# Layer 1's two query products ahead of its keys, the latent stream normalized ahead of layer 0's overflow loop, and one expert job in four f32 passes

## The chip, the core and the metric

The kernel runs on one core of a Trainium2 chip. The metric is device time in microseconds (us), median of several runs; smaller is better. TensorE is called PE here, VectorE DVE, ScalarE ACT, GpSimdE POOL, and SP is the engine whose queue issues most of the loads from HBM.

## What is computed

Two layers act on a residual stream of 256 latent tokens and 256 context tokens, each 1024 wide. The parts that matter here, cut from the reference:

```python
# layer 0: attention and Fourier groups, then a mixture of experts for 512 tokens
ff = moe_ffn(jnp.concatenate([h2, hc2], axis=0), *moe_args)     # 64 experts, top 8, one shared expert
ctx = layer_norm(DN_ALPHA * ctx + cg2 * ff_ctx, ln2_g[l], ln2_b[l])
x = layer_norm(DN_ALPHA * x + g2 * ff_lat, ln2_g[l], ln2_b[l])
# layer 1: neighbourhood attention; the latents ask, latents and context answer
h  = x * (1.0 + sc1) + sh1
hc = ctx * (1.0 + csc1) + csh1
q, k, v = jnp.split(h_lat @ w_in, 3, axis=-1)
kc, vc = jnp.split(h_ctx @ w_in[:, NA_WIDTH:], 2, axis=-1)
```

All arithmetic is in f32 accuracy. Layer 1's queries come from the latents alone (256 columns), its keys and values from latents and context (512 columns).

## The kernel before, in words

**Layer 0's experts.** `moe` walks through 42 jobs (0 to 41) of 128 slots. A job holds one expert (a single), or two (a pair, 64 slots each). Its PE work is the gate and up product (`gate_up`, L1337), the transposes of the next job's input and of its own activation, the down product (`down`, L1351), and scatter matmuls (L1544) that place earlier results at their tokens. Singles after the third job go another way: `gate_up3` and `down3` split each f32 operand into a high part (a cast on ACT) and a low part (a subtraction on DVE), by `split` at L161, and `mm3` (L165 to L167) multiplies in three fp32r passes: high by high, low by high, high by low. The list `passes` says which way a job goes. Job 39 is a single, the last one; jobs 38, 40 and 41 are pairs. The weights come through a pool of 11 tiles of 1 MB (`w8`), which SP's queue refills as PE or DVE let go of them.

**The end of layer 0.** After job 41 four scatter pieces are added to the latents' residual `xt[0:2]` by DVE, `stats` takes their mean and variance, and four scatter pieces of the context are added to `acc[2:4]` by DVE (L1434). `post` brings two slices of layer 1's modulation to column form. Then comes `overflow_blocks`, a loop on the device for experts with more tokens than slots; it runs zero times here, but all engines meet at its branch (L1642). After the loop `normalize` (L1896) brings the latents to their normalized form.

**Layer 1's mixer.** `mixer_na` reads six slices of `na_w_in`: `na[0]`, `na[1]` are the queries of heads 0 to 3 and 4 to 7, `na[2]`, `na[3]` the keys, `na[4]`, `na[5]` the values. `project` multiplies one slice in four steps of 24 matmuls by `mm3`; for each step `prefetch` splits a quarter of the slice (`wh` on ACT, `wl` on DVE) one step ahead, and a `tick` after each step does other work. `turn` transposes a quarter of the stream, scales it (`hTf`, L429 and L430), and splits it (`hT`). The order is: query 0, key 0, value 0, query 1, key 1, value 1. `fold_ctx` (L1889, L1890) and a second `normalize` finish the context beside query 0. `attention` does one unit (a head and half of the queries) for each `next(g)`: a score matmul (L910), softmax on DVE and ACT, four transposes (L493) two units later and four matmuls with the values (L920) one unit after that; its 11 steps for the first four heads lie in the ticks of query 1, key 1 and value 1, one in each.

SP and PE run in the order in which the code is written (`manual_schedule`); DVE, ACT and POOL are ordered by the scheduler.

Of the kernel before, what the change touches and what calls it, by code (L numbers as in the profile page):

```python
# [22 lines left out]
D = 1024  # L23
# [95 lines left out]
def tile_block(ctx: ExitStack, tc: tile.TileContext, I, out):  # L119
# [25 lines left out]
    def k4(shape, name="k4", dt=F32):  # L145
        return keep.tile(shape, dt, name=name, tag="k4", bufs=NK4)
# [366 lines left out]
    def project(w, out_mm, tick, n=4, eng=V, nxt=None, within=None):  # L513


        ps = [bank() for _ in range(n)]
        for jj in range(0, NJ, 2):
            prefetch(w, jj, eng)
            wh, wl = ready_parts.pop((id(w), jj))
            if nxt:  # L520
                if jj + 2 < NJ:
                    prefetch(w, jj + 2, eng)
                elif nxt() is not None:
                    prefetch(nxt(), 0, eng)
            for i in range(n):
                for j in range(2):
                    out_mm(ps[i], i, jj + j, wh[:, j], wl[:, j])
                if within:
                    next(within)
            tick()  # L530
        return ps

    def token_major(h):
        def f(p, i, j, wh, wl):
            sl = slice(i * 128, i * 128 + 128)
            mm3(p, h(0, j, sl), h(1, j, sl), wh, wl, j == 0, j == NJ - 1)
        return f
# [326 lines left out]

    def mixer_na(mp):
        load = na.pop("load")
        na[2], na[4], na[1] = load(2), load(4), load(1)
        st = Stream(2)
        mod_stream(st, 1, range(6, 12), mod_rows,
                   lambda shape: mp.tile(shape, F32, name="mh", tag="mh", bufs=2))  # L870
# [9 lines left out]
        yT = []  # L880
        kv, qT = {}, {}

        def fill(n, steps):

            steps = iter(steps)
            tick = lambda: next(steps)()
            qT[n] = k4([128, 4, 256], "qT")
            ps = project(na[n], channel_major(h, 256), tick, nxt=lambda: na[2 + n])
            del na[n]
            for i in range(4):  # L890
                A.activation(qT[n][:, i], ps[i][:, :256], AF.Copy, scale=SCALE)
            kv[n] = [w8([128, 4, 512], "kv") for _ in range(2)]
            ps = project(na[2 + n], channel_major(h, 512), tick, nxt=lambda: na[4 + n])
            del na[2 + n]
            for i in range(4):
                A.copy(kv[n][0][:, i], ps[i])
            if n == 0:
                na[3] = load(3)
            ps = project(na[4 + n], token_major(h), tick, nxt=lambda: na.get(1))
            del na[4 + n]  # L900
            for i in range(4):
                A.copy(kv[n][1][:, i], ps[i])
            if n == 0:
                na[5] = load(5)
# [30 lines left out]
                    late = attend(*units[i - 2], sms.pop(i - 2))  # L935
                yield

        busy(3)
        for jj in range(2):
            last = turn(0, jj)  # L940
        busy(3)
        prefetch(na[0], 0)
        with tc.issue_after(last[0].ins), tc.issue_after(last[1].ins):
            fold_ctx()
            prefetch(na[0], 2)
            prefetch(na[0], 4, G)
        with tc.issue_after(last[1].ins):
            normalize(Stats(mp, 2).of(xt[2:]), xt[2:])
        order.clear()
        g = attention([(0, hh, t) for hh in range(4) for t in range(2)])  # L950

        def turns(*a):
            for s, jj in a:
                turn(s, jj)
        tail = lambda: next(g, None)
        with tc.issue_after(last[0].ins), tc.issue_after(last[1].ins):
            fill(0, [lambda: turns((0, 2), (0, 3)), lambda: None, lambda: turns((1, 0), (1, 1)),
                     lambda: turns((1, 2), (1, 3))] + [st.tick] * 8)
        del xt[2:]
        yT.extend(k4([128, 4, 256], "yT") for _ in range(2))  # L960

        def both_():
            st.tick()
            tail()
        fill(1, [both_] * 4 + [tail] * 8)
        for _ in g:
            pass
        del kv[0], qT[0]
# [91 lines left out]
    def moe(l, out_of, nt, mp, pre=lambda: None, post=lambda: None):  # L1060
# [356 lines left out]
        def stats():  # L1417

            x_stats.of(xt[0:2], True)
            if l:  # L1420
                y_out.extend(k4([128, D], "y_out") for _ in range(2 - len(y_out)))
                finish1(x_stats, *after, y_out)

        def fold(g2s):
# [216 lines left out]
        def overflow_blocks():  # L1641
            with tc.For_i(0, n_blk.pop()) as i:  # L1642
# [18 lines left out]
                sl1 = mp.tile([128, 1, 5], F32, name="sl1", tag="sl1")  # L1661
                V.tensor_copy(sl1[:, 0], p[:, :5])
                slot_info(sl1, w1, t1, i1)
                x1 = k4([128, D], "x1")
                V.memset(x1, 0.0)
                gather(x1, i1)
                tr = slots_T(x1, 4)
# [7 lines left out]

        passes = []
        for sg_ in jobs:
            passes.append(3 if l == 0 and len(sg_) == 1 and len(passes) > 2 else 4)
        grp, sc = [], iter(())
        over = overflow()  # L1680
        LA = 3 if l == 0 else 2
        with tc.manual_schedule(engines={mybir.EngineType.SP, mybir.EngineType.PE}):
# [186 lines left out]
            if l:  # L1869
                last_job(njob - 1, sc, g2s[0], add_x)  # L1870
                after.extend(spread(lnc[:, k]) for k in range(2))
                stats()
            else:
                for _ in range(4):
                    next(sc)
                stats()
                with tc.issue_after(x_stats.last.ins):
                    for _ in sc:
                        pass
            post()  # L1880

        overflow_blocks()
        return x_stats, y_out

    g2c = []

    def fold_ctx():
        for t in (2, 3):
            V.tensor_mul(acc[t], acc[t], g2c[0])  # L1889
            V.tensor_add(xt[t], xt[t], acc[t])  # L1890
        g2c.clear()
# [41 lines left out]

    mix0.close()
    with tc.tile_pool(name="moe0", bufs=1) as mp:
        normalize(moe(0, out0, 4, mp, preload_na, mods_na)[0], xt[:2])
    with tc.tile_pool(name="mix1", bufs=1) as mp:
        with tc.manual_schedule(engines={mybir.EngineType.SP, mybir.EngineType.PE}):
            out1 = mixer_na(mp)
# [91 lines left out]
```

## Time and profile before

| | us |
|---|---|
| median of 3 runs | 1667.28 (1667.20 to 1667.38) |
| the profiled execution's own time | 1667.79 |
| its span | 1666.0 |
| PE busy | 1560.8 (94%) |
| DVE, ACT, POOL busy | 762.9, 444.3, 174.0 |
| moved by DMA | 547.91 MB, 329 GB/s over the span |

Layer 0's experts end at about 936 us of the span, where the loop's branch is; layer 1's mixer goes on to about 1100, and layer 1's experts to the end. The profiled execution took 0.5 us more than the median. Busy times of a matmul are modelled, so spacings between matmuls are read from their starts. An f32 matmul shows as two records, an fp32r matmul as one.

### The profile page before, as it was taken

What the parts mean: (1) busy time and instruction counts of PE and PEld (TensorE: products, weight loads), DVE (VectorE), ACT (ScalarE), POOL (GpSimd) and SP (SyncE); (2) the same over time, 40 slices, a digit from 0 to 9 for tenths busy, and PEclk for the clock granted to TensorE, in tenths of its full rate; (3) what the DMA queues carried; (4) which work ended last, traced back from release to release, by engine and by line L of the source; (5) the groups of instructions that cost most, each with busy time, mean ns of one, the idle gap of its engine ahead of it and who ended that gap; (6) DMA issues with size and microseconds to landing.
All of it is one profiled execution on the core that took longest, in us unless ns stands there. A gap on an engine that the chain in (4) does not pass through costs nothing. (4 is left out here: it accounts for less than half of the span.)

```text
span 1666.0 us, 30733 instructions
## 1 busy us (share of the span) xinstructions
PE 1560.8 (94%) x12138; PEld 1005.9 (60%) x12138; DVE 762.9 (46%) x2077; ACT 444.3 (27%) x882; POOL 174.0 (10%) x162
## 2 busy tenths in 40 slices
PE   7999999999999999999998799999999988989995
PEld 5765687546556566565665577866756654546542
DVE  2475585425455445354566832347443422223225
ACT  2447311113132232232222243332222211112111
POOL 1003210123221121221110000011000000000000
PEclk9999999999999999999999899999999999999998
DMA  9947864799999999989998566247779999999994
GB/s 331 340 172 290 297 233 162 268 366 382 346 398 345 402 401 389 392 327 406 404 407 309 205 212 222 89 181 309 303 316 420 419 419 419 419 420 419 419 420 179
DMA packets 122819, 547.91 MB, mean 329 GB/s; under 512 B 12917, under 2 KB 21509, under 8 KB 74672
## 3 DMA queue, kind: packets, MB, share of 16 engines
q1 hardware_dynamic: 108032, 501.76, 75.6%
q0 software_dynamic: 14640, 44.15, 8.6%
q8 instruction: 97, 1.59, 0.4%
q14 instruction: 50, 0.41, 0.1%
HBM read 532.10 MB, written 21.58 MB: 332 GB/s over the span
## 5 line engine op out<-in xcount | busy, mean ns | idle before, releaser
L1337 PE MATMUL bank<-w,xT 128*32 128x256 f32 (+1 forms) x5696 | 462.8, 388 | 25.8 <-DMA w<-in_moe_w_up_dram 20.2
L1337 PEld LDWEIGHTS bank<-w,xT 128*32 128x32 f32 (+1 forms) x5696 | 276.5, 122 | 204.9 <-DMA w<-in_moe_w_up_dram 28.2
L1351 PE MATMUL bank<-w,aT 128*32 128x512 f32 (+2 forms) x1248 | 235.3, 599 | 3.0 <-ACT aT L1312 2.9
L1293 DVE SCALAR_TENSOR_TENSOR a<-s,wsl,bank 128x256 f32<-128x256 f32 x70 | 33.6, 480 | 407.4 <-ACT s L1292 407.4
L1292 ACT ACTIVATE s<-bank 128x256 f32<-128x256 f32 x70 | 26.9, 385 | 544.5 <-PE bank L1337 496.7
L1544 PE MATMUL bank<-yy,ss 128*128 128x512 f32 x560 | 159.0, 411 | 1.4 <-DVE yy L161 1.1
L1536 DVE TENSOR_TENSOR acc<-acc,bank 128x512 f32<-128x512 f32 x212 | 138.0, 683 | 43.3 <-PE bank L1544 41.6
L1351 PEld LDWEIGHTS bank<-w,aT 128*32 128x32 f32 (+2 forms) x1248 | 68.5, 123 | 120.0 <-issue 104.0
L1544 PEld LDWEIGHTS bank<-yy,ss 128*128 128x128 f32 x560 | 97.3, 191 | 25.9 <-DVE yy L161 5.0
L161 DVE TENSOR_TENSOR yy<-bank,yy 128x512 fp32r<-128x512 f32 x96 | 65.9, 689 | 91.7 <-ACT yy L161 91.7
L161 ACT CAST yy<-bank 128x512 fp32r<-128x512 f32 x96 | 56.2, 586 | 161.6 <-PE bank L1351 144.2
L1445 POOL DMA_INDIRECT xg<-h2d,idx x42 | 52.1, 1239 | 356.8 <-PE bank L1459 181.7
L161 DVE TENSOR_TENSOR wl<-half,wh 128x1024 fp32r<-128x1024 f32 x35 | 42.7, 1224 | 74.4 <-ACT wh L161 74.4
L1250 DVE TENSOR_SCALAR oh<-ib,pos 128x64 bf16<-128x64 bf16 (+3 forms) x432 | 68.7, 245 | 9.7 <-PE bank L1276 9.7
L1516 POOL DMA_INDIRECT accd<-yd,idx x37 | 59.4, 1605 | 128.0 <-issue 92.7
L165 PE MATMUL bank<-wh,hT 128*128 128x512 f32 x160 | 65.2, 407 | 1.7 <-ACT wh L161 1.1
L167 PE MATMUL bank<-wl,hT 128*128 128x512 f32 x160 | 63.4, 396 | 0.5 <-DVE wl L161 0.5
L166 PE MATMUL bank<-wh,hT 128*128 128x512 f32 x160 | 63.2, 395 | 0.3 <-DVE hT L161 0.2
L1485 PE MATMUL bank<-ohr,h2p 128*128 128x256 f32 x448 | 60.8, 289 | 0.0
L1485 PEld LDWEIGHTS bank<-ohr,h2p 128*128 128x128 f32 x448 | 55.3, 191 | 8.2 <-PE bank L1337 4.4
L1437 POOL TENSOR_TENSOR xr<-xr,tmp 128x512 f32<-128x512 f32 x2 | 3.3, 1649 | 478.2 <-DVE tmp L1436 478.2
L1459 PE MATMUL bank<-head,xg 128*128 128x128 f32 x336 | 52.1, 278 | 0.0
(362 smaller groups left out, 2313.2 us busy)
## 6 DMA issues: line engine op xcount, KB each, us to landing
w<-in_moe_w_gate_dram SPq DMA_DIRECT2D x128, 1024.0 KB
w<-in_moe_w_up_dram SPq DMA_DIRECT2D x128, 1024.0 KB
w<-in_moe_w_down_dram SPq DMA_DIRECT2D x104, 1024.0 KB
w<-in_w_mod_dram SPq DMA_DIRECT2D x24, 1024.0 KB
half<-in_na_w_in_dram SPq DMA_DIRECT2D x12, 1024.0 KB
mh<-in_w_mod_dram SPq DMA_DIRECT2D x12, 1024.0 KB
w<-in_w_mod_dram SPq DMA_DIRECT2D x16, 512.0 KB
row<-rowsd POOLq DMA_DIRECT2D x15, 512.0 KB, 8.3
```

The lines of the kernel that those rows point to most:

```text
L161: return A.copy(o_h, src), eng.tensor_sub(o_l, src, o_h.bitcast(F32))
L165: T.matmul(p, xh, wh, start=first, stop=False)
L166: T.matmul(p, xl, wh, start=False, stop=False)
L167: T.matmul(p, xh, wl, start=False, stop=last)
L1250: V.tensor_scalar(oh[:, 32 * lane:32 * (lane + m)], ib[:, off:off + 32 * m], pos[:, t, c:c + 1], None, op0=OP.is_equal)
L1337: T.matmul(p[sl, q * FF:q * FF + FF], xT(j, sl), ws[k][0][q][:, j], start=j == 0, stop=j == NJ - 1, **kw)
L1351: T.matmul(p[sl], aT[:, j, sl], d[:, n * 512:n * 512 + 512], start=j == 0, stop=j == 1, **kw)
L1445: G.indirect_dma_start(out=x, out_offset=None, in_=h2d[:n2, :], in_offset=bass.IndirectOffsetOnAxis(ap=idx_col, axis=0), bounds_check=n2 - ...
L1485: T.matmul(o, h2p[t][k][:, 2 * q + j], oh[:, t].rearrange("p a b -> p (a b)")[:, :n], start=t == 0 and k == 0, stop=t == nt - 1 and k == 1)
L1516: G.indirect_dma_start(out=accd[turn_[0]][:, :], out_offset=bass.IndirectOffsetOnAxis(ap=i_, axis=0), in_=y[32 * lane:32 * (lane + m)], in ...
L1536: add = {0: lambda t, r, p: V.tensor_add(acc[t][:, r], acc[t][:, r], p)}
L1544: T.matmul(p, ss[:, t * 128:t * 128 + 128], yy[:, q, r], start=k == 0 and q == 0, stop=k == len(grp) - 1 and q == 1)
```

## The change

- `passes`: the last three jobs are no longer eligible for three passes, so job 39 runs as `gate_up` and `down` in plain f32 (four passes inside PE), without splits of its input, weights and activation.
- The end of layer 0: the context's four last pieces are copied by ACT from PSUM to a tile `late` of the pool `w8`; `post` comes ahead of `stats`; `stats` also writes the normalized latents to two new tiles `y_out`, ahead of the loop, which take the place of `xt[0:2]`. `fold_ctx` adds `late` to `acc` first. In the loop's body `x1` moves to another pool.
- The mixer: `fill` loses its query product to `queries`. The order is now query 0, query 1, key 0, value 0, key 1, value 1; the loads of slices follow it. `fold_ctx` and the context's `normalize` come after the first step of query 0, with a square root on ACT in place of one on DVE; the first context quarters are turned in the ticks of query 1. Three warm-up matmuls go, and no split is given to POOL any more. In value 1 each tick takes two attention steps (`two_tails`).

```diff
-        na[2], na[4], na[1] = load(2), load(4), load(1)
+        na[1], na[2], na[4] = load(1), load(2), load(4)
...
-        def fill(n, steps):
+        def queries(n, steps, nxt):
 
             steps = iter(steps)
-            tick = lambda: next(steps)()
             qT[n] = k4([128, 4, 256], "qT")
-            ps = project(na[n], channel_major(h, 256), tick, nxt=lambda: na[2 + n])
+            ps = project(na[n], channel_major(h, 256), lambda: next(steps)(), nxt=lambda: na[nxt])
             del na[n]
             for i in range(4):
                 A.activation(qT[n][:, i], ps[i][:, :256], AF.Copy, scale=SCALE)
+
+        def fill(n, steps):
+
+            steps = iter(steps)
+            tick = lambda: next(steps)()
...
-            ps = project(na[4 + n], token_major(h), tick, nxt=lambda: na.get(1))
+            ps = project(na[4 + n], token_major(h), tick, nxt=lambda: na.get(3))
...
-        busy(3)
         for jj in range(2):
             last = turn(0, jj)
         busy(3)
         prefetch(na[0], 0)
         with tc.issue_after(last[0].ins), tc.issue_after(last[1].ins):
-            fold_ctx()
             prefetch(na[0], 2)
-            prefetch(na[0], 4, G)
-        with tc.issue_after(last[1].ins):
-            normalize(Stats(mp, 2).of(xt[2:]), xt[2:])
...
+        def rest():
+
+            turn(0, 2)
+            last = turn(0, 3)
+            with tc.issue_after(last[1].ins):
+                fold_ctx()
+                normalize(Stats(mp, 2).of(xt[2:], True), xt[2:])
...
-            fill(0, [lambda: turns((0, 2), (0, 3)), lambda: None, lambda: turns((1, 0), (1, 1)),
-                     lambda: turns((1, 2), (1, 3))] + [st.tick] * 8)
+            queries(0, [rest, none, none, none], 1)
+        queries(1, [none, none, lambda: turns((1, 0), (1, 1)), lambda: turns((1, 2), (1, 3))], 2)
+        fill(0, [st.tick] * 8)
...
-        fill(1, [both_] * 4 + [tail] * 8)
+
+        def two_tails():
+            tail()
+            tail()
+        fill(1, [both_] * 4 + [two_tails] * 4)
...
-            if l:
-                y_out.extend(k4([128, D], "y_out") for _ in range(2 - len(y_out)))
+            y_out.extend(k4([128, D], "y_out") for _ in range(2 - len(y_out)))
+            if l == 0:
+                for t in range(2):
+                    mu, rs = x_stats[t]
+                    V.tensor_scalar(y_out[t], xt[t], mu, rs, op0=OP.subtract, op1=OP.mult)
+            else:
                 finish1(x_stats, *after, y_out)
...
-            passes.append(3 if l == 0 and len(sg_) == 1 and len(passes) > 2 else 4)
+            passes.append(3 if l == 0 and len(sg_) == 1 and 2 < len(passes) < njob - 3 else 4)
...
+                add_x = add[0]
+                late.append(w8([128, 2, D], "late"))
+                add[0] = lambda t, r, p: A.copy(late[0][:, t - 2, r], p)
+                for _ in sc:
+                    pass
+                add[0] = add_x
+                post()
                 stats()
-                with tc.issue_after(x_stats.last.ins):
-                    for _ in sc:
-                        pass
-            post()
 
         overflow_blocks()
+        if l == 0:
+            xt[:2] = y_out
...
     def fold_ctx():
+        y = late.pop()
         for t in (2, 3):
+            V.tensor_add(acc[t], acc[t], y[:, t - 2])
             V.tensor_mul(acc[t], acc[t], g2c[0])
             V.tensor_add(xt[t], xt[t], acc[t])
...
-        normalize(moe(0, out0, 4, mp, preload_na, mods_na)[0], xt[:2])
+        moe(0, out0, 4, mp, preload_na, mods_na)
```

What this does to the engines' orders is seen at three places. The first is PE in job 39. In the program before, its down product is twelve matmuls that alternate between the parts (`wh`, `wl` of the weights, `aTh`, `aTl` of the activation):

```order
L1544 MATMUL bank<-yy,ss 128x512 x4
L165 MATMUL bank<-wh,aTh 128x512
L166 MATMUL bank<-wh,aTl 128x512
L167 MATMUL bank<-wl,aTh 128x512
L165 MATMUL bank<-wh,aTh 128x512
...
L1544 MATMUL bank<-yy,ss 128x512 x8
```

In the changed program the whole job reads so on PE:

```order
L1350 MATMUL bank<-w_8772,xT 128x256 x8
L1350 MATMUL bank<-w_8774,xT 128x256 x8
L1476 MATMUL bank<-head,xg_1854 128x128 x4
L1561 MATMUL bank<-yy,ss 128x512 x4
L1321 MATMUL bank<-head,a 128x128 x2
L1476 MATMUL bank<-head,xg_1854 128x128 x4
L1561 MATMUL bank<-yy,ss 128x512 x4
L1364 MATMUL bank<-w_8776,aT 128x512 x4
L1561 MATMUL bank<-yy,ss 128x512 x8
```

Forty-eight matmuls of the gate and up product have become 16, and twelve of the down product four; the transposes and scatters between them stand as they did.

The second place is DVE right after the loop's branch. Before, it starts with the latents' normalization and has the context's fold (L1889, L1890) ahead of query 0's second low part:

```order
L1896 TENSOR_SCALAR xr_9103<-xr_9103,mv,rs 128x1024
L1896 TENSOR_SCALAR xr_9105<-xr_9105,mv,rs 128x1024
L161 TENSOR_TENSOR wl<-half,wh 128x1024
L430 TENSOR_SCALAR hTf<-bank,acol_1807,bcol_1808 128x256 x2
L161 TENSOR_TENSOR hT<-hTf,hT 128x2x256 x2
L1889 TENSOR_TENSOR acc_2623<-acc_2623,row 128x1024
L1889 TENSOR_TENSOR acc_2754<-acc_2754,row 128x1024
L1890 TENSOR_TENSOR xr_9107<-xr_9107,acc_2623 128x1024
L1890 TENSOR_TENSOR xr_9109<-xr_9109,acc_2754 128x1024
L161 TENSOR_TENSOR wl<-half,wh 128x1024
```

In the changed program:

```order
L161 TENSOR_TENSOR wl<-half,wh 128x1024
L430 TENSOR_SCALAR hTf<-bank,acol_1807,bcol_1808 128x256 x2
L161 TENSOR_TENSOR hT<-hTf,hT 128x2x256 x2
L161 TENSOR_TENSOR wl<-half,wh 128x1024 x3
L430 TENSOR_SCALAR hTf<-bank,acol_1807,bcol_1808 128x256 x2
L161 TENSOR_TENSOR hT<-hTf,hT 128x2x256 x2
L1912 TENSOR_TENSOR acc_2623<-acc_2623,late 128x1024
...
L1914 TENSOR_TENSOR xr_9041<-xr_9041,acc_2754 128x1024
...
L459 BN_STATS st<-xr_9041 128x6
L161 TENSOR_TENSOR wl<-half,wh 128x1024
```

All four low parts of query 0 and all four turned quarters of the latents now stand ahead of the fold; the last `wl` shown is the first low part of query 1, and it stands behind six 1024-wide operations of the fold and four statistics.

The third place is PE in value 1, after its first step, where a tick takes two attention steps (`ps` is a softmax's result, `PT` its transpose on ACT, `kv` the keys or values):

```order
L914 MATMUL bank_10404<-kv_9818,qT_9496 128x512
L924 MATMUL bank_10414<-PT_10361,kv_9819 128x128 x4
L493 MATMUL bank_10421<-head_69,ps_10296 128x128 x4
L914 MATMUL bank_10427<-kv_9818,qT_9496 128x512
L924 MATMUL bank_10437<-PT_10420,kv_9819 128x128 x4
L493 MATMUL bank_10444<-head_69,ps_10347 128x128 x4
```

The transposes of `ps_10296` fill the bank from which `PT_10420` is copied, and the second step's four value matmuls read that copy with one score matmul between; `ps_10347` belongs to the score of the tick before.

## Rows read from the trace of the kernel before

**Rows 1.** The page, moved bytes in 40 equal slices of the span.

```profile
GB/s 331 340 172 290 297 233 162 268 366 382 346 398 345 402 401 389 392 327 406 404 407 309 205 212 222 89 181 309 303 316 420 419 419 419 419 420 419 419 420 179
```

**Rows 2.** Windows: length, PE, PEld, DVE, ACT, POOL busy, PEclk, DMA share, GB/s.

```profile
847.23:862.92 15.69, 15.69 (x107) 9.67 (x107) 9.95 (x17) 5.27 (x9) 2.13 (x3) 1.00 1.02 421
862.92:887.72 24.80, 18.31 (x88) 15.32 (x86) 16.88 (x22) 6.42 (x10) 1.05 (x2) 0.79 0.87 344
907.12:935.93 28.81, 22.18 (x139) 10.90 (x138) 20.36 (x37) 4.97 (x10) 0.00 (x0) 0.91 0.36 133
935.93:963.38 27.45, 21.94 (x139) 20.00 (x140) 23.05 (x43) 12.65 (x21) 3.19 (x1) 0.84 1.01 376
963.38:1100.00 136.62, 136.62 (x731) 103.20 (x730) 43.95 (x78) 47.60 (x83) 1.09 (x2) 1.00 0.43 148
```

**Rows 3.** Timeline of PE in job 39: start, length, instructions [idle before, releaser].

```profile
866.37 0.58 PE L167 MATMUL bank<-wl,xT 128*128 128x256 f32 x1 [3.06 <-DVE wl L161]
878.31 0.49 PE L166 MATMUL bank<-wh,aTl 128*128 128x512 f32 x1 [1.60 <-DVE aTl L161]
880.64 0.80 PE L167 MATMUL bank<-wl,aTh 128*128 128x512 f32 x1 [1.83 <-DVE wl L161]
```

**Rows 4.** Timeline of DVE in job 39.

```profile
865.09 2.36 DVE L161 TENSOR_TENSOR wl<-w,wh 128x1024 fp32r<-128x1024 f32 x2
```

**Rows 5.** Timeline of PE in layer 1's shared expert, f32 products of one expert's shape.

```profile
1148.26 7.13 PE L1389 MATMUL bank<-w,h2T 128*128 128x256 f32 x32
1161.68 3.60 PE L1351 MATMUL bank<-w,aT 128*128 128x512 f32 x8
```

**Rows 6.** Windows, columns as above.

```profile
880.00:890.00 10.00, 9.36 (x40) 6.89 (x42) 5.49 (x8) 1.17 (x2) 0.00 (x0) 0.67 0.42 145
```

**Rows 7.** The tile ad (context sums fetched from DRAM): issue to landing.

```profile
DMA to landing us min/median/max: 14.8/14.8/14.8
```

**Rows 8.** Timeline around the loop's branch; the last row is from the kernel's end.

```profile
932.36 2.47 DVE L1434 TENSOR_TENSOR acc<-acc,bank 128x512 f32<-128x512 f32 x4
935.62 1.04 ACT L161 CAST wh<-half 128x1024 fp32r<-128x1024 f32 x1 [4.00 <-DVEq L1642]
935.93 1.65 PE L274 MATMUL bank<-onesf 128*128 128x128 f32 x6 [3.79 <-DVEq L1642]
937.03 1.53 DVE L1896 TENSOR_SCALAR xr<-xr,mv,rs 128x1024 f32<-128x1024 f32 x2 [2.20 <-ACT wh L161]
937.90 0.48 PE L425 MATMUL bank<-head,xr 128*128 128x128 f32 x1 [0.32 <-DVE xr L1896]
...
1649.12 2.05 ACT L394 COPY spread<-bank 128x512 f32<-128x512 f32 x4 [2.22 <-PE bank L393]
```

**Rows 9.** Timeline of DVE after the loop.

```profile
940.16 0.54 DVE L430 TENSOR_SCALAR hTf<-bank,acol,bcol 128x256 f32<-128x256 f32 x1 [0.46 <-ACT hTf L429]
941.52 1.42 DVE L161 TENSOR_TENSOR hT<-hTf,hT 128x512 fp32r<-128x512 f32 x2
942.85 2.35 DVE L1889 TENSOR_TENSOR acc<-acc,row 128x1024 f32<-128x1024 f32 x2
948.53 1.87 DVE L459 BATCH_NORM_STATS2 st<-xr 128x6 f32<-128x512 f32 x3
```

**Rows 10.** Timeline of PE in query 0, at its second step.

```profile
948.67 0.39 PE L166 MATMUL bank<-hT,wl 128*128 128x256 f32 x1 [2.52 <-DVE wl L161]
```

**Rows 11.** Timeline of PE in query 1: first and last of the 24 matmuls of a step.

```profile
1017.93 0.39 PE L165 MATMUL bank<-hT,wh 128*128 128x256 f32 x1
1020.79 0.28 PE L167 MATMUL bank<-hT,wh 128*128 128x256 f32 x1
```

**Rows 12.** Groups by line in 940 to 1230, the longest steps of an attention unit.

```profile
L484 ACT ACTIVATE ps<-bank,mx 128x512 f32<-128x512 f32 x16 | 11.1, 692 | 10.4 <-DVE mx L483 7.3 <-issue 3.1
L482 DVE TENSOR_REDUCE mx<-bank 128x1 f32<-128x512 f32 x16 | 11.0, 690 | 0.4
L494 ACT COPY PT<-bank 128x512 f32<-128x512 f32 x16 | 9.4, 586 | 6.1 <-PE bank L493 6.1
```

More of the change, by code (lines that the diff above doesn't have):

```diff
@@ L881, in mixer_na @@
         kv, qT = {}, {}
+        def queries(n, steps, nxt):
+            steps = iter(steps)
+            qT[n] = k4([128, 4, 256], "qT")
+            ps = project(na[n], channel_major(h, 256), lambda: next(steps)(), nxt=lambda: na[nxt])
+            del na[n]
+            for i in range(4):
+                A.activation(qT[n][:, i], ps[i][:, :256], AF.Copy, scale=SCALE)
         def fill(n, steps):
@@ L886, in fill @@
             tick = lambda: next(steps)()
-            qT[n] = k4([128, 4, 256], "qT")
-            ps = project(na[n], channel_major(h, 256), tick, nxt=lambda: na[2 + n])
-            del na[n]
-            for i in range(4):
-                A.activation(qT[n][:, i], ps[i][:, :256], AF.Copy, scale=SCALE)
             kv[n] = [w8([128, 4, 512], "kv") for _ in range(2)]
@@ L955, in mixer_na @@
         tail = lambda: next(g, None)
+        def rest():
[4 more added lines that the diff above has]
+                normalize(Stats(mp, 2).of(xt[2:], True), xt[2:])
+        none = lambda: None
         with tc.issue_after(last[0].ins), tc.issue_after(last[1].ins):
-            fill(0, [lambda: turns((0, 2), (0, 3)), lambda: None, lambda: turns((1, 0), (1, 1)),
-                     lambda: turns((1, 2), (1, 3))] + [st.tick] * 8)
+            queries(0, [rest, none, none, none], 1)
+        queries(1, [none, none, lambda: turns((1, 0), (1, 1)), lambda: turns((1, 2), (1, 3))], 2)
+        fill(0, [st.tick] * 8)
         del xt[2:]
@@ L1663, in overflow_blocks @@
                 slot_info(sl1, w1, t1, i1)
-                x1 = k4([128, D], "x1")
+                x1 = t8([128, D], "x1", F32)
                 V.memset(x1, 0.0)
@@ L1875, in moe @@
                     next(sc)
+                add_x = add[0]
[5 more added lines that the diff above has]
+                post()
                 stats()
-                with tc.issue_after(x_stats.last.ins):
-                    for _ in sc:
-                        pass
-            post()
         overflow_blocks()
+        if l == 0:
+            xt[:2] = y_out
         return x_stats, y_out
-    g2c = []
+    g2c, late = [], []
     def fold_ctx():
+        y = late.pop()
         for t in (2, 3):
+            V.tensor_add(acc[t], acc[t], y[:, t - 2])
             V.tensor_mul(acc[t], acc[t], g2c[0])
```

## The prediction

> **What bounds the kernel now.** First the 40 slices of the page. From slice 31 on, the chip moves a steady 420 GB/s: layer 1's experts wait for their weights. In slices 22 to 28 it drops to 89 to 309 [rows 1]: there the transfers wait for the engines, so time that the engines gain there starts layer 1's stream of weights earlier and reaches the end. Then windows cut at the change's places [rows 2]. Job 38, a pair, has PE busy in all of its 15.69 us. Job 39, the single in three passes, takes 24.80, with PE busy 18.31 and a mean granted clock of 0.79. From the start of job 41 to the branch PE has gaps as well (busy 22.18 of 28.81), and in the 27.45 us from the branch to key 0 it is busy 21.94, while DVE is busy 23.05. From key 0 to 1100 PE has no gap at the full clock, and DVE is busy in a third of it. So the path runs through PE; where PE waits, it is for DVE, at three places: job 39, the branch, and query 0. The change touches these three, and moves attention steps into the stretch without a gap.
>
> Times are summed against the profiled execution, 1667.79 us; the median of the runs is 0.5 lower.
>
> **Job 39.** What it loses today is in PE's rows: it waits 3.06 us for the low part of the first weights, 1.60 for that of the activation, 1.83 for the down weights' [rows 3], each low part after its cast at 2.36 for two on DVE [rows 4]. In f32 no part is made. Sixteen gate and up matmuls of this very shape took 7.13 us in the shared expert, four down matmuls 3.60 [rows 5]. The order of instructions shows that all else in the job stays, and it is what pair jobs have: transposes, eight scatter matmuls, the down product, eight more. Job 38 has a product of equal length in the array (a pair's two halves run side by side) and the same remainder in 15.69 us without a gap [rows 2]. I take that for the single: 24.80 - 15.69 = **9.1 us saved**. DVE also loses six weight parts of 1.2 us and some smaller ones, so it is not late next.
>
> What could be late next is data. The weights of jobs 40 and 41 are asked for when PE or DVE lets go of earlier ones; at 880 to 890 the DMA share falls to 0.42 [rows 6] from 1.02 in job 38 [rows 2], so by about 882 all that had been asked for had landed, while job 41 would begin near 898 instead of 907.12. Job 40's weights stand ahead of 4 MB of job 41's in the queue, which take about 10 us at 0.42 MB per us, so they are there by about 872 and job 40 begins near 878.6. The last sums fetched from DRAM land 14.8 us after their issue [rows 7], at about 873, and DVE would like them at 871. The bank copies queued behind them on DVE would be up to 2.5 us late; PE meets that only if it runs out of banks, so 0 to 1.5 us. Bounds for the job: 7.6 to 9.6 saved.
>
> The Trainium skill (FP8 and Floating Point Precision, section TensorE Precision Notes) says that true FP32 takes four passes through the array and that reduced-precision FP32 is one reading of a truncated value; by that four passes should cost a third more PE time than three. The rows agree for the PE time that remains when nothing is waited for, and disagree with it as a forecast for the job, whose three passes waited for their parts.
>
> **Up to the branch.** DVE's last work there, four adds of the context, takes 2.47 us from 932.36 [rows 8]. They become four copies on ACT; I price these by four ACT copies of the same size from PSUM, 2.05 us [rows 8]. DVE gets instead the latents' normalization, 1.53, moved from behind the branch, and two reductions of 0.15 that stood ahead of it. So DVE ends near 934.2 instead of 934.8. ACT was idle for 4.00 us before its first cast behind the branch [rows 8], so it had ended by 931.6; with one modulation copy of 0.6 and four of 2.05 to do after its square root it ends near 934.3, as late as DVE. **0.5 us saved**; bounds 0.8 saved to 0.8 lost, as ACT may now resume as slowly as DVE did, whose first instruction came 1.1 after PE's [rows 8].
>
> **From the branch to key 0, with query 1.** Before: 27.45 us [rows 2], and query 1 comes later, at 2.87 us for 24 matmuls [rows 11], 11.5 for its four steps: 38.95 together. After, counted from PE's first instruction behind the branch: the transposes need no normalization and start at 0.3 instead of 1.97, but DVE's first low part stands behind a cast of 1.04 [rows 8], so the first matmul of query 0 comes at about 4.5 (before 5.6). Query 0 then needs 11.5 plus one for eight transposes and half a us for `hT`: done at 17.5. DVE meanwhile resumes at about 2, makes four low parts (1.2 each), scales four quarters (0.54 each) and makes four `hT` low parts (0.7 each), with about a us of waits: 12.3 [rows 4, 9]. Then the fold in three pairs of 2.35, four statistics at 0.62, and only then query 1's first low part: 12.3 + 7.05 + 2.6 + 1.2 = 23.2 [rows 9]. PE waits from 17.5 to 23.2. Query 1 (11.5) and 16 transposes (2.0) follow, and the clock will have fallen: in job 39, after the wait of 3.06, the matmuls start 0.22 apart, the lower of the two levels, 1.2 GHz, where 0.12 is usual at 2.4 GHz; its 14 slow starts cost 1.4 us. I add 1.1. Key 0 begins at 37.8: **1.1 us saved**. The fold that delayed query 0's second step by 2.52 [rows 10] now delays query 1's first by more, so most of the gain of an earlier start is given back. Bounds: 4 saved if DVE's chain is faster than my sum and the clock holds, 3 lost if DVE is 2 us slower and the clock stays low through half of query 1.
>
> **Attention.** Eleven steps go through twelve calls as before, four of one and four of two. PE's work is the same. In a doubled tick the second step's value matmuls want a transpose that was issued one score matmul (about 0.85 us) earlier and a copy of 0.59 on ACT [rows 12]: a tenth of a us of waiting each, and about 0.7 in the last tick, where no score is left to lie between. **0.8 us lost**, bounds 0 to 2.5.
>
> Costed at nothing: the loads' new order (query 1's slice is used ten us or more after its landing would be; transfers then have a share of 0.43 [rows 2]); `late`'s place in the pool, given back by the fold long before key 0 ends; the three warm-up matmuls, which lie in PE's wait. If key 0 or later loads came late they would show as new PE gaps in a stretch that has none.
>
> **Sum.** -9.1 - 0.5 - 1.1 + 0.8 = -9.9: 1657.9 for the profiled execution, **1657.4** for the median. A difference under 0.2%, 3.3 us, can't be told from no change here.
>
> **Rivals.**
> 1. *The gain of job 39 is eaten by transfers.* Layer 0's jobs run at a DMA share of 1.02 [rows 2]; were job 40 to start only when it does now, 9.1 falls away and the rest gives 1667.28 - 0.8 = 1666.5. Against it: the queue ran empty at 882 [rows 6]. Chance 0.04.
> 2. *Query 1 runs at the low clock throughout.* Its 96 matmuls would cost 0.1 us more each, 9.6, in place of 1.1: 1665.9. For it, a wait of 5.7 us, longer than the 3.06 after which the clock fell in job 39 [rows 3]; against it, that fall lasted 3 us. Chance 0.03.
> 3. *Slower: doubled ticks make the attention units wait on themselves.* The place is value 1, four ticks. If a unit's transposes had to wait for its own softmax, PE would wait for at least the maximum, the exponential and the copy, 0.69 + 0.69 + 0.59 = 2.0 us [rows 12], and with the bias, scaling and transposes of the same unit about 3.5; for eight units 28, less the 0.8 counted: 1684.6. It decides for no gain from 1.3 us per unit, and is over the 0.2% line from 1.75. Against it: the order shows transposes that read softmaxes of the tick before; banks are the way in which it could still come, as four are held by the product. Chance 0.05.
> 4. *Four passes cost more, the splits were hidden.* Then the job changes by 7.13 + 3.60 - 48 x 0.12 - 12 x 0.22 = +2.3, and the time is 1668.8. Against it stand the gaps of rows 3. Chance 0.02.
>
> **How the numbers follow.** The forecast has 0.86. Its terms' bounds give -9.6 - 0.8 - 4 = -14.4 to -7.6 + 0.8 + 3 + 2.5 = -1.3 if all fall on one side; four in five of the weight lies in -13.5 to -5.3, so **1653.8 to 1662**. Faster by over 0.2%: the forecast and little else, 0.88; within 0.2%: rivals 1, 2 and 4 and the upper end of the bounds, 0.07; slower: rival 3, 0.05.
>
> **What would show it.** Right: job 39 takes 15 to 17 us without a wait for `wl`; DVE and ACT reach the branch together; PE has one gap of 4 to 7 us at query 1's second matmul, released by DVE, with a lower granted clock behind it; key 0 to the end of value 1 without gaps of a us. Wrong: new waits of PE for DMA in jobs 40 and 41, gaps in value 1 released by ACT, or layer 1's weights that start no earlier.

## The result and the profile after

The changed kernel takes 1657.88 us (median of five runs, 1655.95 to 1660.63) against 1667.28 (1666.22 to 1667.83): ratio 0.9941, interval 0.9929 to 0.9953. The forecast was 1657.4. A second set gave 0.9962 (0.9947 to 0.9977). Single executions of one kernel lie up to 11 us apart (run 3 below), so the stretches of the traces decide small things here, and the times only the large ones.

Windows of the changed kernel, columns as in [rows 2]: job 39, job 40, job 41 to the first matmul behind the branch, from there to key 0, key 0 to the end of value 1:

```profile
863.83:879.04 15.21, 15.21 (x67) 11.44 (x65) 8.26 (x14) 3.10 (x6) 0.00 (x0) 1.00 1.01 413
879.04:898.46 19.42, 19.42 (x124) 12.49 (x123) 11.10 (x20) 3.10 (x6) 0.00 (x0) 1.00 1.02 399
898.46:924.54 26.08, 20.49 (x139) 10.50 (x138) 19.45 (x35) 6.60 (x13) 0.00 (x0) 1.00 0.41 152
924.54:963.73 39.19, 32.04 (x230) 31.41 (x231) 28.71 (x40) 18.59 (x30) 0.00 (x0) 0.87 0.73 269
963.73:1086.38 122.65, 121.97 (x616) 88.55 (x614) 36.03 (x64) 42.54 (x74) 1.06 (x2) 1.00 0.47 163
```

The last stretch in the kernel before, which held query 1 (key 0's first matmul starts at 963.41, 0.03 behind the cut of [rows 2]):

```profile
963.41:1096.44 133.03, 133.03 (x712) 100.56 (x710) 41.17 (x68) 46.98 (x82) 1.09 (x2) 1.00 0.44 152
```

Job 39 went from 24.80 to 15.21 us, as busy and as gapless as a pair. Job 41 to the branch went from 28.81 to 26.08. Branch to key 0 grew by 11.71 and now holds query 1; the last stretch shrank by 10.38. Taken together the mixer takes 1.33 us more than before in these two traces; the table below shows that one program's mixer differs by as much between executions.

PE's timeline in job 39 has not one wait:

```profile
863.83 7.07 PE L1350 MATMUL bank<-w,xT 128*128 128x256 f32 x32
...
873.68 3.59 PE L1364 MATMUL bank<-w,aT 128*128 128x512 f32 x8
876.71 2.40 PE L1561 MATMUL bank<-yy,ss 128*128 128x512 f32 x8
879.04 7.13 PE L1350 MATMUL bank<-w,xT 128*64 128x256 f32 x64
```

The 10 us reach layer 1. SP issues its first load of that layer's experts stage 10.00 us earlier, in the kernel before and after:

```profile
1103.62 0.35 SPq L1100 DMA_DIRECT2D cst<-in_cols_dram  x1
```

```profile
1093.62 0.35 SPq L1113 DMA_DIRECT2D cst<-in_cols_dram  x1
```

From the end of value 1 to the end of the span it is 569.6 us before (1666.0 - 1096.44) and 569.3 after (1655.7 - 1086.38): all that was gained ahead of layer 1's experts was kept. In the change's second trace it is 570.9 (1657.2 - 1086.27): layer 1's first job took 36.86 there instead of 35.37, at a mean granted clock of 0.95 instead of 1.00.

PE's timeline at the branch and at query 1's second matmul:

```profile
924.54 1.09 PE L425 MATMUL bank<-head,y_out 128*128 128x128 f32 x8 [2.48 <-DVEq L1659]
...
928.12 0.38 PE L165 MATMUL bank<-hT,wh 128*128 128x256 f32 x1 [1.81 <-ACT hT L161]
...
948.07 0.58 PE L166 MATMUL bank<-hT,wl 128*128 128x256 f32 x1 [5.11 <-DVE wl L161]
948.45 0.41 PE L167 MATMUL bank<-hT,wh 128*128 128x256 f32 x1
948.66 0.41 PE L165 MATMUL bank<-hT,wh 128*128 128x256 f32 x1
...
953.93 0.28 PE L166 MATMUL bank<-hT,wl 128*128 128x256 f32 x1
```

The wait of 5.11 us is the one forecast, and behind it the starts are 0.21 apart until 953.78: the lower of the two levels. DVE's timeline says what it was doing meanwhile, the fold, the statistics and only then the low part:

```profile
937.54 2.36 DVE L1912 TENSOR_TENSOR acc<-acc,late 128x1024 f32<-128x1024 f32 x2
939.81 2.35 DVE L1913 TENSOR_TENSOR acc<-acc,row 128x1024 f32<-128x1024 f32 x2
942.08 2.35 DVE L1914 TENSOR_TENSOR xr<-xr,acc 128x1024 f32<-128x1024 f32 x2
944.35 1.87 DVE L459 BATCH_NORM_STATS2 st<-xr 128x6 f32<-128x512 f32 x3
...
946.80 1.21 DVE L161 TENSOR_TENSOR wl<-half,wh 128x1024 fp32r<-128x1024 f32 x1
```

In value 1 one row waits, the last of the doubled ticks:

```profile
1078.50 1.16 PE L924 MATMUL bank<-PT,kv 128*128 128x128 f32 x8 [0.68 <-ACT PT L494]
```

### The profile page after: what moved, and what is told of

Its sections match the earlier page's. It is cut to its first block, busy times and chain, and to the rows that moved or that the text cites. A ratio compares the mean times of both kernels' runs of the same rounds, so it can differ in the third digit from the quotient of the medians.

```text
span 1655.7 us, 30672 instructions
## 1 busy us (share of the span) xinstructions
PE 1558.8 (94%) x12112; PEld 1003.8 (61%) x12112; DVE 753.8 (46%) x2059; ACT 441.0 (27%) x881; POOL 170.9 (10%) x161
## 5 line engine op out<-in xcount | busy, mean ns | idle before, releaser
L1350 PE MATMUL bank<-w,xT 128*32 128x256 f32 (+2 forms) x5728 | 473.5, 391 | 22.0 <-DMA w<-in_moe_w_up_dram 18.1
L1350 PEld LDWEIGHTS bank<-w,xT 128*32 128x32 f32 (+2 forms) x5728 | 286.1, 124 | 202.0 <-issue 31.0
```

What stands on the lines that cost most here:

```text
L1350: T.matmul(p[sl, q * FF:q * FF + FF], xT(j, sl), ws[k][0][q][:, j], start=j == 0, stop=j == NJ - 1, **kw)
```

## The experiments

My theory from these traces: job 39 gives the whole gain, the rest about nothing, because the early query 1 pays for DVE's fold with a wait and with slow matmuls. The rivals: the parts need each other; the mixer carries a share; the wait cannot be removed, only moved.

All runs in one table: ratio to before with its interval, and in us the same stretches of each run's trace as in the windows above.

| run | ratio (95%) | job 39 | job 41 to branch | branch to key 0 | key 0 to end of value 1 |
|---|---|---|---|---|---|
| before | | 24.80 | 28.81 | 27.48 | 133.03 |
| the change, first trace | 0.9941 (0.9929 to 0.9953) | 15.21 | 26.08 | 39.19 | 122.65 |
| the change again | 0.9962 (0.9947 to 0.9977) | 15.23 | 26.08 | 39.20 | 122.65 |
| 1: job 39 only | 0.9953 (0.9937 to 0.9968) | 15.22 | 28.53 | 27.58 | 133.00 |
| 2: without job 39 | 1.0018 (1.0009 to 1.0028) | 24.87 | 28.70 | 39.63 | 122.64 |
| 3: mixer as before | 0.9960 (0.9946 to 0.9974) | 15.22 | 26.09 | 27.60 | 133.01 |
| 4: low parts first | 0.9955 (0.9942 to 0.9968) | 15.22 | 27.71 | 38.37 | 123.37 |
| 5: all in four passes | 0.9918 (0.9901 to 0.9936) | 15.22 | 26.08 | 37.81 | 122.66 |
| 6: fold between | 0.9940 (0.9923 to 0.9956) | 15.23 | 26.02 | 33.54 | 122.96 |
| 7: and one step a tick | 0.9931 (0.9916 to 0.9946) | 15.23 | 27.72 | 34.24 | 121.90 |
| 8: 5 and 7 together | 0.9874 (0.9856 to 0.9891) | 15.21 | 26.08 | 33.41 | 123.51 |
| 9: before, all in four passes | 0.9892 (0.9872 to 0.9913) | 15.22 | 28.53 | 28.71 | 133.01 |

The last two columns hold chance of 1.1 to 1.6 us. From job 41 to the end of value 1, runs 1 and 9 have the same instructions, and so have the change and run 5, and runs 7 and 8. Yet from the branch to key 0 runs 1 and 9 took 27.58 and 28.71, the change again and run 5 took 39.20 and 37.81, and from key 0 on runs 7 and 8 took 121.90 and 123.51. The windows of the change again and of run 5:

```profile
924.42:963.62 39.20, 31.98 (x231) 31.18 (x231) 28.71 (x40) 18.53 (x30) 0.00 (x0) 0.87 0.72 269
912.94:950.75 37.81, 31.75 (x231) 30.84 (x231) 28.72 (x40) 18.64 (x30) 0.00 (x0) 0.86 0.75 279
```

PE waits 5.09 us at query 1's second matmul in both, and the mean granted clock is nearly equal, but it fell at other places: run 5 has 21 slow starts behind the wait and no run of them in query 0's first step, where the change again has 24 and 16. So one trace of each order does not tell the old mixer from the new one: the old took 160.5 to 161.7 from the branch to the end of value 1 (before, runs 1, 3 and 9), the change's 160.5 to 162.3 (the change twice, runs 2 and 5).

**1. Job 39 only.**

```diff
-            passes.append(3 if l == 0 and len(sg_) == 1 and len(passes) > 2 else 4)
+            passes.append(3 if l == 0 and len(sg_) == 1 and 2 < len(passes) < njob - 3 else 4)
```

> The kernel before with one edit: job 39 in plain f32. By the sum of the parts as the changed kernel's trace corrects it (job 39 -9.6 us, everything behind it merely earlier) the time is 9.6 us below before, ratio 0.9942, with job 39 at 15.2 us and layer 1's first expert loads about 10 us earlier. The rival, that job 39's gain only reaches the end because the mixer was rearranged too (layer 1's loads wait for something else by then), gives less than half of it: 4 us or less, ratio above 0.9975. Second question: from the start of job 41 to the first matmul behind the branch the change saved 2.73 us. If its new order did that, this run still takes 28.8 us there; if 1.7 of it was job 41's down product that happened to run at the lower clock in the trace of before, it takes 27.1 with that product at 3.65 us instead of 5.35.

The interval holds the 0.9942, and the rival's 0.9975 lies outside it. One line gives what the whole change gives; its gain needs nothing else to reach the end. On the second question the trace shows 28.53, with the down product of job 41 at 5.35 us as in the kernel before.

**2. The change without job 39**: that line put back in the changed kernel.

> The changed kernel with job 39 put back to three passes. By the corrected sum (-2.7 or, without the clock's part, -1.0 up to the branch; +1.3 from the branch to the end of value 1) it is 1.4 us below before to 0.3 above, ratio 0.9992 to 1.0002. By my forecast's terms (-0.5, -1.1, +0.8) it is 0.8 below, 0.9995: the two can't be told apart by the time, only by the stretches. The rival, that the rearranged mixer carries a real share of the 9.4 us, gives a ratio of 0.9975 or less.

Slower than before by 0.9 to 2.8 parts in a thousand, 1.5 to 4.7 us, so the rest of the change costs time when it stands alone; both sums were too kind to it. The stretches of the table that it changes add up to 190.97 (28.70 + 39.63 + 122.64) against 189.32 before, 1.65 more; that is within the chance of these stretches, so it is the interval of the times that shows the cost.

**3. The mixer as before**: the changed kernel with `mixer_na` taken from the kernel before.

> The changed kernel with the mixer's order of before (query 1 behind value 0, one attention step a tick, the fold beside query 0's second step); job 39 and the new end of layer 0 stay. If the rearranged mixer costs the 1.3 us that the stretch from the branch to the end of value 1 grew by, this is 1 us faster than the change, less up to 0.8 because the fold has two more adds ahead of query 0's second low part: ratio to before 0.9934 to 0.9941. If the rearrangement gains the 0.3 us of my forecast, it is 0.3 slower, 0.9943. If it gains much more than that (clock or transfers elsewhere), this kernel is above 0.9960. PE should wait 2.5 to 3.5 us at query 0's second step and nowhere for query 1.

The interval (0.9946 to 0.9974; its runs went from 1655.79 to 1666.6) does not tell the cases apart; the ratio lies just outside both narrow expectations and on the edge of the third. The stretches do: branch to the end of value 1 takes 160.61, against 160.51 before and 161.84 in the change. So the old order takes 1.2 us less here, which is within the chance of these stretches (run 5 has 160.47 with the change's order): which of the two is better is not shown. Its wait at query 0's second step grew beyond the 2.5 to 3.5 I had put down, to 4.66 from the 2.52 of [rows 10]:

```profile
937.43 0.58 PE L166 MATMUL bank<-hT,wl 128*128 128x256 f32 x1 [4.66 <-DVE wl L161]
```

**4. Low parts first.** The cut of the edit:

```diff
-            with tc.issue_after(last[1].ins):
-                fold_ctx()
-                normalize(Stats(mp, 2).of(xt[2:], True), xt[2:])
+        def half_fold():
+            with tc.issue_after(order["parts"][1].ins):
+                next(fold, None)
+        def norm():
+            with tc.issue_after(order["parts"][1].ins):
+                normalize(Stats(mp, 2).of(xt[2:], True), xt[2:])
...
-            queries(0, [rest, none, none, none], 1)
-        queries(1, [none, none, lambda: turns((1, 0), (1, 1)), lambda: turns((1, 2), (1, 3))], 2)
+            queries(0, [rest, none, none, half_fold], 1)
+        queries(1, [half_fold, none, norm, last_turns], 2)
```

> The changed kernel with the context's fold, statistics and normalization taken from in front of query 1's low parts on DVE: half of the fold behind the first low part, the rest between the next ones, all four context turns after query 1's last step. If the 5.1 us wait at query 1's second matmul and the 26 slow matmuls behind it are what the early query 1 costs, the wait falls under 1 us, the clock stays at 2.4 GHz through query 1, and key 0 starts 5 to 7 us earlier after the branch: 1651 to 1653 where the change has 1657.9, ratio to before 0.990 to 0.9915. The rival, that the wait only moves (to key 0, for the context's normalization, or to a transfer), leaves the time within 2 us of the change, ratio 0.993 to 0.995.

The rival was right: the time is 1657.84, the ratio 0.9955, just above the rival's 0.995, and the stretch 38.37 us. The 5.11 is gone, and PE's timeline waits at key 0 instead:

```profile
956.83 0.48 PE L425 MATMUL bank<-head,xr 128*128 128x128 f32 x1 [3.14 <-DVE xr L1932]
957.55 3.46 PE L425 MATMUL bank<-head,xr 128*128 128x128 f32 x15 [0.24 <-DVE xr L1932]
961.32 0.79 PE L165 MATMUL bank<-hT,wh 128*128 128x512 f32 x1 [0.31 <-ACT hT L161]
```

On DVE three low parts of key 0 had come ahead of the context's normalization (L1932), 3.7 us of them:

```profile
951.43 1.21 DVE L161 TENSOR_TENSOR wl<-half,wh 128x1024 fp32r<-128x1024 f32 x1
...
952.98 1.23 DVE L161 TENSOR_TENSOR wl<-half,wh 128x1024 fp32r<-128x1024 f32 x1
...
954.82 1.22 DVE L161 TENSOR_TENSOR wl<-half,wh 128x1024 fp32r<-128x1024 f32 x1
955.96 1.53 DVE L1932 TENSOR_SCALAR xr<-xr,mv,rs 128x1024 f32<-128x1024 f32 x2
```

**5. All jobs in four passes**: `passes.append(4)` in the changed kernel.

> The changed kernel with the other seven three-pass jobs in plain f32 too. In the trace of before the eight three-pass jobs had 19.5 us of PE waits for their parts, 6.5 of them in job 39; the four passes take 2.3 us more each at full clock. If these waits count as they did in job 39, the seven give 13.0 - 16.1 = 3 us lost to, with the time at the low clock that goes with the waits (about 1.4 us each), 7 gained. If the stream of weights sets the pace there (DMA share 1.02 in the jobs around), nothing is gained or lost: within 2 us of the change. My theory for job 39 says why it was different: it is the last three-pass job, by then the queue ran empty, so I expect the second.

I expected nothing; it is 8.2 us faster than the change measured beside it (1650.37 against 1658.55). Windows of the jobs 20, 15 and 29, in this order, in the kernel before, in the change, and in this run:

```profile
591.27:604.47 13.20, 12.22 (x84) 10.36 (x81) 10.28 (x18) 5.82 (x9) 5.24 (x3) 1.00 1.03 389
517.16:534.41 17.25, 14.50 (x96) 12.39 (x92) 12.28 (x26) 6.31 (x10) 1.93 (x1) 0.90 0.93 382
716.43:730.68 14.25, 12.51 (x78) 10.46 (x78) 10.18 (x12) 7.00 (x10) 1.94 (x1) 1.00 0.84 337
```

```profile
590.71:603.90 13.19, 12.21 (x84) 10.36 (x80) 10.28 (x18) 5.82 (x9) 5.24 (x3) 1.00 1.03 390
518.10:533.85 15.75, 12.99 (x96) 10.90 (x92) 12.27 (x26) 6.30 (x10) 1.93 (x1) 1.00 0.93 384
715.87:731.60 15.73, 13.97 (x79) 11.95 (x79) 10.17 (x12) 7.00 (x10) 1.95 (x1) 0.89 0.76 308
```

```profile
582.38:595.86 13.48, 13.48 (x64) 10.04 (x60) 4.76 (x12) 2.51 (x5) 3.97 (x3) 1.00 1.02 389
511.56:525.53 13.97, 13.97 (x76) 10.49 (x72) 5.90 (x19) 3.02 (x6) 1.02 (x1) 1.00 0.99 414
706.25:719.74 13.49, 13.49 (x61) 10.05 (x59) 3.68 (x6) 3.10 (x6) 1.02 (x1) 1.00 0.97 400
```

In job 20, whose parts are nearly in time, four passes cost 0.28 us. In jobs 15 and 29 they save 1.8 to 3.3 and 0.8 to 2.2, because three passes left waits of 1.7 to 2.8 us and, in one of the two traces each, a stretch at the lower clock. The seven jobs together take 100.75 us in the change's second trace and 94.74 here. Another 2.6 us lies in the jobs just ahead of three of them: jobs 5, 10 and 28 take 13.89, 13.39 and 15.42 in the change's second trace and 13.45, 12.97 and 13.69 here, and the same here as in runs 8 and 9. There PE waited for ACT, which had the casts of the next job to make; job 29's first matmul, where job 28's window ends, waits 1.66 us in the change:

```profile
715.87 0.39 PE L165 MATMUL bank<-wh,xT 128*128 128x256 f32 x1 [1.66 <-ACT wh L161]
```

The two together are 8.6 us, against 8.2 between the medians; set against the trace of before, whose seven jobs took 99.24, they would be 7.1. A DMA share of 0.93 to 1.03 did not mean that PE waited for data.

The Trainium skill (FP8 and Floating Point Precision, section TensorE Precision Notes) makes true FP32 four products of high and low halves; by that, as an estimate, the three passes should need three quarters of PE's time. The trace shows less of a saving: job 20's gate and up product takes 5.82 us in three passes (591.27 to the next instruction at 597.09) and 6.99 in four (582.38 to 589.37), a ratio of 0.83. Over the job PE is busy 12.22 and 13.48 us, scatters and transposes included, so 1.3 us are saved, and the waits for parts took most of it or more. The prediction's "the rows agree" with a third more for four passes holds only roughly: its own rows give 10.73 to 8.40, 1.28 times, and this product 1.20 times.

**6. The fold between.** From run 4: the fold's first two operations behind query 0's third low part, the others behind query 1's first, the statistics behind its third.

```diff
-            queries(0, [rest, none, none, half_fold], 1)
-        queries(1, [half_fold, none, norm, last_turns], 2)
+            queries(0, [rest, half_fold, none, half_fold], 1)
+        queries(1, [none, norm, none, last_turns], 2)
```

> As the run with the low parts first, but the fold's first two operations go into DVE's idle time during query 0 (2.9 us of waiting for a free buffer), the statistics stand behind query 1's third low part, and only one low part of key 0 is ahead of the context's normalization where there were three (3.7 us of DVE time). If DVE's chain to the context's normalization is what the wait moved to (3.14 us before the context's transposes), it now ends about 5 us earlier, PE has no wait over 1 us from query 0's second step to key 0, and branch to key 0 takes 33 to 35 us (38.4 there, 39.2 in the change): 4 to 6 us faster than the change. If instead the wait comes back at another place (low parts of query 1 for lack of buffers, or transfers), 37 us or more, and no gain.

33.54 us, inside the 33 to 35. The time is 1654.71 against 1658.55, 3.8 less, with intervals that still overlap; the stretch is 5.7 less than in the change's two traces and 4.3 less than in run 5, which has the change's order, so more than its chance. DVE does two of the fold's operations where it had been idle, in its timeline:

```profile
931.38 1.22 DVE L1922 TENSOR_TENSOR acc<-acc,late 128x1024 f32<-128x1024 f32 x1
932.63 1.23 DVE L1923 TENSOR_TENSOR acc<-acc,row 128x1024 f32<-128x1024 f32 x1
```

One wait is left at key 0, for ACT's cast of the turned stream, in PE's timeline:

```profile
954.03 1.91 PE L425 MATMUL bank<-head,xr 128*128 128x128 f32 x16
957.55 0.50 PE L165 MATMUL bank<-hT,wh 128*128 128x512 f32 x1 [1.61 <-ACT hT L161]
```

I had said no wait over 1 us; this one is 1.61.

**7. One step a tick.** From run 6:

```diff
-        fill(0, [st.tick] * 8)
+        fill(0, [st.tick] * 5 + [both_] * 3)
...
-        fill(1, [both_] * 4 + [two_tails] * 4)
+        fill(1, [both_] * 4 + [tail] * 4)
```

> The run before it plus attention's first three steps in the last three ticks of value 0, so that no tick takes two steps. The doubled ticks cost 0.68 us of waiting in the last tick; from key 0 to the end of value 1 it should take 121.9 to 122.0 us instead of 122.65, and the time 0.7 us less than the run before it. A rival: a score that stands earlier makes ACT or DVE late for value 0's own splits, and the stretch does not shorten.

The stretch takes 121.90 without a gap. The time is 1.0 us lower, which these intervals cannot tell from nothing; branch to key 0 took 0.7 more at a lower granted clock (0.86 against 0.95). Run 8, with the same order, took 123.51 in the stretch, at a mean granted clock of 0.82 in its first 9.3 us, so the 0.7 us is shown as a wait that is gone, not as time.

**The change again.**

> The changed kernel itself once more, beside the next three on one chip. Its program's own stretches should repeat to 0.2 us: job 39 15.2, from the branch's first matmul to key 0 about 39.2, from key 0 to the end of value 1 122.65. The open point is job 41's down product, 3.65 us in the change's first trace and 5.35 in that of before, of the run with job 39 alone, of the run without it, and of the run with the low parts first, but 3.65 in the run with the old mixer. If it hangs on chance in an execution, this trace may show either; if the change's order decides it, 3.65 again. The ratio to before should be near 0.994 to 0.9955.

All stretches repeat within 0.02 us, and job 41's down product takes 3.65 again. Runs 6 and 7 answer the open point: their programs are the same up to value 0, and PE's timeline shows job 41's down product behind the same waits at either level, in run 6 and in run 7:

```profile
906.21 0.50 PE L1331 MATMUL bank<-head,a 128*128 128x128 f32 x2 [1.09 <-DVE a L1316]
907.46 3.65 PE L1374 MATMUL bank<-w,aT 128*64 128x512 f32 x16 [0.75 <-ACT aT L1335]
```

```profile
906.79 0.51 PE L1326 MATMUL bank<-head,a 128*128 128x128 f32 x2 [1.09 <-DVE a L1311]
908.05 5.35 PE L1369 MATMUL bank<-w,aT 128*64 128x512 f32 x16 [0.75 <-ACT aT L1330]
```

**8 and 9. The two gains together, and the one line alone.** Run 8 is run 7 with `passes.append(4)`; run 9 is the kernel before with it.

> The two gains together: the run with the fold between and one attention step a tick, and all jobs of layer 0 in plain f32. They lie in different stretches, so they should add: 8.2 us below the change from the jobs and 4.8 from the mixer, 13 in all, ratio to before 0.988 to 0.9895 (about 1646). If the seven jobs' gain was only the clock's chance in the executions of that run, this is no better than the mixer's part alone: ratio 0.992 or more.

> The kernel before with one edit: no job in three passes. By job 39 (-9.6) and the other seven (about -8, of which 6 were seen in these jobs themselves and the rest in the clock of jobs beside them) 1648 to 1651, ratio 0.988 to 0.991, so as fast as the change with the same edit or faster: the rearranged mixer and the new end of layer 0 together were measured at about nothing. If the change's other two parts do gain something after all, this run is at least 2 us slower than the change with the same edit (0.9918).

Run 8 took 1645.92 us against 1667.74, a little below the 0.988 to 0.9895 expected: the gains add, and it beats both kernels, by 1.3% and by 0.7 to 0.9% (0.9874 against 0.9941 and 0.9962). Run 9 took 1649.72, ratio 0.9892; the change with the same line had 0.9918, with overlapping intervals. So in the form in which the change has them, its mixer and its end of layer 0 gain nothing that can be measured, and run 2 has them cost 1.5 to 4.7 us. With the fold between, run 8 is 3.8 us ahead of run 9; their intervals overlap too, but from job 41 to the end of value 1 it needs 183.00 against 190.25. Of these 7.25 us, 1.7 are the level of job 41's down product in the two executions, and 2.0 are lost again behind value 1 (571.7 against 569.7 to the end of the span), 1.5 of them in layer 1's first job (36.85 against 35.37), which runs at either level in the change's two traces as well. So the fold between is shown to shorten its stretch; how much of that the kernel's time keeps is not.

## Why the prediction was right

- **Job 39**, forecast 9.1 saved: 9.59. The remainder was what a pair has, the transfers did not come late (rival 1: PE waits for no DMA in jobs 40 and 41), and four passes did not cost more here (rival 4). I took the pair's 15.69 for it; it was 15.21: behind the first matmul of its down product the next scatter starts 3.03 us later (873.68 to 876.71), in job 40 it is 3.58. Run 1 shows the whole of it with this edit alone.
- **Up to the branch**, forecast 0.5 saved, bounds 0.8 to -0.8: 2.73 in the profiled executions, outside. About 1.7 of it is job 41's down product (5.35 to 3.65 us), which runs 6 and 7 show to be chance of an execution. With the slow product on both sides the new end takes 27.71 and 27.72 (runs 4 and 7) against 28.53 and 28.81 with the old: 0.8 to 1.1 saved. Run 2 has 28.70 with the new end: PE waits 0.85 us there for a modulation copy on ACT, where it is 0.38 in the change. ACT's order differs there: its four `late` copies, from 927.37, stand ahead of the second modulation copy at 929.28, while in the change that copy comes first (920.79, then `late` from 921.25).
- **Branch to key 0 with query 1**, forecast 37.8, 1.1 saved: 39.19, and by the step prices of the forecast (27.48 + 11.47 for query 1, 4 x 24 matmuls 0.1195 apart) 0.24 lost. The mechanism was right and its wait nearly (5.11 for 5.7). DVE's chain was well met too: the fold began 13.0 behind the branch (937.54 - 924.54) for 12.3, where the forecast's own terms with "about a us of waits" add up to 12.8, and the low part of query 1 ended at 23.5 (948.01) for 23.2. The term for the clock was too small for this execution. I had taken 14 slow starts from job 39; there were 26 behind the wait, up to 953.78, and 13 in query 0's first step, behind the branch, that I had not put down. At 0.094 each that is 3.7 for 1.1. An earlier first matmul (3.6 after the branch's first for 4.5) gave some of it back. Run 5, with 21 slow starts in the same instructions, took 37.81, the forecast's own figure, so the size of this term is chance of an execution. Rival 2, the low clock in all 96, did not come.
- **Attention**, forecast 0.8 lost: 1.09 (122.65 against 133.03 - 11.47), 0.68 of it in the last doubled tick, where 0.7 had been put. Rival 3 did not come: no other tick waits, as the transposes read the softmaxes of the tick before.
- **The sum** of 9.9 was met (1667.79 to 1657.88 for the profiled executions) partly by luck: the clock's 1.7 us at job 41 made up for the mixer, which is 1.6 us worse than forecast in this trace. That 1.7 us has its opposite ahead of anything the change touches: job 39 began 0.9 later in that execution, as jobs 11, 15 and 29 took 1.5 more (last section) and what lies ahead of job 6 took 0.6 less. Without both, job 39 and the end of layer 0 came out 0.5 and up to 0.6 us better than forecast, and the mixer worse.

What the forecast did not see is where the same reasoning led: it priced three passes against four for job 39 only, while of the other seven such jobs four (6, 11, 15 and 29) lost to the same waits; the three whose parts were nearly in time (20, 25 and 34) are 0.1 to 0.3 us faster in three passes (run 5). And it named the fold as the thing that query 1 waits for without drawing the conclusion that the order, and not the amount of DVE's work, was the cost (runs 4 and 6).

## What to carry to other kernels

A split that saves a pass on TensorE pays only if its parts are ready: add the waits for them, and the slower matmuls behind those waits, to the shorter product before calling it faster. When a product is moved to an earlier place, list what stands ahead of its operands on the engine that makes them; moving that work behind the first operand is not enough if it then delays the next stage, so place it in an idle gap. And measure the parts of a bundled change apart: here one line of it held the gain.

## What the runs showed of the hardware

The granted clock is not repeatable between executions of one program: job 41's down product took 3.65 or 5.35 us behind the same two waits, and job 15 and job 29, the same program in the kernel before and in the change, took 17.25 and 14.25 us in one trace and 15.75 and 15.73 in the other. So a single profile can be off by 1.7 us in a stretch without any cause in the code.

These levels go together. The nine traces with the seven three-pass jobs show only two sets for jobs 11, 15, 29 and job 41's down product: 14.0, 17.2, 14.2 and 5.35 us (before, runs 1, 2, 4 and 7), or 15.5, 15.8, 15.7 and 3.65 (the change twice, runs 3 and 6). The second set is 1.5 us longer in the jobs and 1.7 shorter at job 41, so over the kernel the two nearly cancel. What picks the set no run here shows.

The mean granted clock of a stretch is not enough to compare two traces: 39.20 and 37.81 us of the same instructions had 0.87 and 0.86. What differed was whether the low level fell on the product's matmuls or, in run 5, on the transposes at the branch and the wait behind them; that is seen by counting the slow starts.
